# A rotary embedding on one core: three loads on SyncE's queue, and the software ring behind the sine table

## The chip, the cores and the metric

The kernel runs on 1 core of a Trainium2 chip. The metric is the device time of one execution in microseconds (us), as the median of several runs; a profile of one execution shows what each engine and each DMA queue did. The engines named here are VectorE (DVE), ScalarE (ACT), GpSimd (POOL) and SyncE (SP); TensorE has no work.

## The reference

The inputs are x of 8 x 2048 x 16 x 64 (batch, position, head, channel) and two tables of 2048 x 32, all float32. Each head's 64 channels are two halves that are rotated by the angle of the position:

```python
x1 = x[..., :head_dim // 2]
x2 = x[..., head_dim // 2:]
cos = cos[None, :, None, :]
sin = sin[None, :, None, :]
out1 = x1 * cos - x2 * sin
out2 = x1 * sin + x2 * cos
return np.concatenate([out1, out2], axis=-1)
```

So 67.1 MB are read and as many are written, for three elementwise operations on each element.

## The kernel before

One batch is one tile `xt` of 128 partitions. A partition holds J = 16 consecutive positions ("rows" here) of 16 heads and 64 channels, 16384 elements of float16. Five such buffers go round (`NBUF = 5`). GpSimd loads a batch with a DMA that turns float32 into float16 on its way (`load`, L54), VectorE rotates it in place with three operations of the whole tile (`rotate`: the product with sine at L75 into a scratch tile `v`, the product with cosine at L81, the sum at L83), and GpSimd stores it with a DMA that turns it back into float32 (`store`, L62; `store_rows`, L108). All of GpSimd's DMAs go through one software queue, q0 in the profile, which works them off in the order of issue. The kernel calls this order the ring, and writes it out by hand with order-only dependencies: load 0, the store of one row of batch 0, loads 1 to 4, and then stores and later loads in turn. A later load waits until the store of its buffer's last contents has landed.

The start is arranged by itself. The first two rows of batch 0 (`JA = 2`, the tile `head`, 1 MB in all) do not come with load 0 but as float32 by ScalarE's hardware queue (L44), behind the cosine table (L43); the sine table comes by SyncE's (L42). Load 0 brings the other 14 rows and waits for nothing. ScalarE narrows the tables to float16: sine into the upper half of `sin_h` (L94), its negative into the lower half (L95), cosine into `cos_h` (L96); then the head's first row and its second (`narrow_head`, L89, two calls). VectorE rotates the first row alone (`JF = 1`), GpSimd stores it (L108), and only behind that store come loads 1 to 4, of which the last takes the buffer that `head` had. The other 15 rows of batch 0 are rotated once load 0 has landed.

At the end, batch 7 goes out in three pieces: nine rows and five rows by GpSimd (L136, L138), and two rows that ScalarE widens (L147) and SyncE sends (L148) once the nine rows have landed.

Of the kernel before, what the change touches and what calls it, by code (L numbers as in the profile page):

```python
# [1 line left out]

# [4 lines left out]


@with_exitstack  # L10
def kernel(
    ctx: ExitStack,
    tc: tile.TileContext,
    x: bass.AP,
    cos: bass.AP,
    sin: bass.AP,
    out: bass.AP,
):
    nc = tc.nc
    f16 = mybir.dt.float16  # L20
    f32 = mybir.dt.float32

    B, S, H, D = x.shape
    Dh = D // 2
    P = nc.NUM_PARTITIONS
    J = S // P
    NBUF = 5

    const_pool = ctx.enter_context(tc.tile_pool(name="rope_const", bufs=1))
    io_pool = ctx.enter_context(tc.tile_pool(name="rope_io", bufs=NBUF))  # L30
    tmp_pool = ctx.enter_context(tc.tile_pool(name="rope_tmp", bufs=1))

    JA = 2
    JE = 2
    JF = 1
    head = io_pool.tile([P, JA, H, D], f32, tag="xt")
    x0 = x[0].rearrange("(p j) h d -> p j (h d)", j=J)
    sin_f = const_pool.tile([P, J, Dh], f32)
    cos_f = const_pool.tile([P, J, Dh], f32)
    cos_h = const_pool.tile([P, J, Dh], f16)  # L40
    sin_h = const_pool.tile([P, J, D], f16)
    nc.sync.dma_start(out=sin_f, in_=sin.rearrange("(p j) d -> p j d", j=J))  # L42
    nc.scalar.dma_start(out=cos_f, in_=cos.rearrange("(p j) d -> p j d", j=J))  # L43
    nc.scalar.dma_start(  # L44
        out=head.rearrange("p j h d -> p (j h d)"),
        in_=x0[:, 0:JA, :].rearrange("p j f -> p (j f)"),
    )

    loads = []

    def load(b):
        xt = io_pool.tile([P, J, H, D], f16, tag="xt")
        j0 = JA if b == 0 else 0
        dma = nc.gpsimd.dma_start(  # L54
            out=xt[:, j0:J, :, :].rearrange("p j h d -> p (j h d)"),
            in_=x[b].rearrange("(p j) h d -> p j (h d)", j=J)[:, j0:J, :].rearrange("p j f -> p (j f)"),
        )
        loads.append(dma)
        return xt

    def store(b, xt, j0=0):
        return nc.gpsimd.dma_start(  # L62
            out=out[b].rearrange("(p j) h d -> p j (h d)", j=J)[:, j0:J, :].rearrange("p j f -> p (j f)"),
            in_=xt[:, j0:J, :, :].rearrange("p j h d -> p (j h d)"),
        )

    def rotate(xt, j0, j1):
        v = tmp_pool.tile([P, J, H, D], f16)
        n = j1 - j0
        js = slice(j0, j1)  # L70
        shape = [P, n, H, 2, Dh]
        sin_b = sin_h[:, js, :].rearrange("p j (e d) -> p j e d", e=2).unsqueeze(2).to_broadcast(shape)
        cos_b = cos_h[:, js, :].unsqueeze(2).to_broadcast([P, n, 2 * H, Dh])
        xe = xt[:, js, :, :].rearrange("p j h (e d) -> p j h e d", e=2)
        nc.vector.tensor_mul(  # L75
            out=v[:, js, :, :].rearrange("p j h (e d) -> p j h e d", e=2),
            in0=xe[:, :, :, ::-1, :],
            in1=sin_b,
        )
        xw = xt[:, js, :, :].rearrange("p j h (e d) -> p j (h e) d", d=Dh)  # L80
        nc.vector.tensor_mul(out=xw, in0=xw, in1=cos_b)  # L81
        xa = xt[:, js, :, :].rearrange("p j h d -> p (j h d)")
        nc.vector.tensor_add(out=xa, in0=xa, in1=v[:, js, :, :].rearrange("p j h d -> p (j h d)"))  # L83


    tiles = [load(0)]

    def narrow_head(j0, j1):
        nc.scalar.copy(  # L89
            out=tiles[0][:, j0:j1, :, :].rearrange("p j h d -> p (j h d)"),  # L90
            in_=head[:, j0:j1, :, :].rearrange("p j h d -> p (j h d)"),
        )

    nc.scalar.copy(out=sin_h[:, :, Dh:D], in_=sin_f)  # L94
    nc.scalar.mul(out=sin_h[:, :, 0:Dh], in_=sin_f, mul=-1.0)  # L95
    nc.scalar.copy(out=cos_h, in_=cos_f)  # L96
    narrow_head(0, JF)
    narrow_head(JF, JA)
    rotate(tiles[0], 0, JF)
    def part(b, j0, j1):  # L100
        return (
            out[b].rearrange("(p j) h d -> p j (h d)", j=J)[:, j0:j1, :].rearrange("p j f -> p (j f)"),
            tiles[b][:, j0:j1, :, :].rearrange("p j h d -> p (j h d)"),
        )

    def store_rows(b, j0, j1):
        dst, src = part(b, j0, j1)
        return nc.gpsimd.dma_start(out=dst, in_=src)  # L108

    first = store_rows(0, 0, JF)  # L110
    ring = [loads[0], first]
    for b in range(1, NBUF):
        tiles.append(load(b))
        ring.append(loads[b])
    for a, b in zip(ring[1:], ring[:-1]):
        tc.add_manual_dep(
            a.ins,
            b.ins.name,
            mybir.DependencyInfo(mybir.DependencyClass.NoSync, mybir.DependencyReason.DATA),
            reason="order of the ring",  # L120
        )
    for b in range(B):
        rotate(tiles[b], JF if b == 0 else 0, J)
        if b < B - 1:
            st = store(b, tiles[b], JF if b == 0 else 0)
            if b == 0:
                tc.add_manual_dep(
                    st.ins,
                    first.ins.name,
                    mybir.DependencyInfo(mybir.DependencyClass.NoSync, mybir.DependencyReason.DATA),  # L130
                    reason="order of the ring",
                )
        if b + NBUF < B:
            tiles.append(load(b + NBUF))
    dst, src = part(B - 1, 0, 9)
    gate = nc.gpsimd.dma_start(out=dst, in_=src)  # L136
    dst, src = part(B - 1, 9, J - JE)
    rest = nc.gpsimd.dma_start(out=dst, in_=src)  # L138
    tc.add_manual_dep(
        rest.ins,  # L140
        gate.ins.name,
        mybir.DependencyInfo(mybir.DependencyClass.NoSync, mybir.DependencyReason.DATA),
        reason="order of the ring",
    )
    dst, src = part(B - 1, J - JE, J)
    tail = io_pool.tile([P, JE, H, D], f32, tag="xt")
    nc.scalar.copy(out=tail.rearrange("p j h d -> p (j h d)"), in_=src)  # L147
    end = nc.sync.dma_start(out=dst, in_=tail.rearrange("p j h d -> p (j h d)"))  # L148
    tc.add_manual_dep(
        end.ins,  # L150
        gate.ins.name,
        mybir.DependencyInfo(mybir.DependencyClass.Sync, mybir.DependencyReason.DATA),
        reason="the last rows go out behind this part",
    )


# [1 line left out]
_INS = ['x', 'cos', 'sin']  # L158
_OUTS = [((8, 2048, 16, 64), 'float32')]


# [23 lines left out]
```

## Time and profile before

| | us |
|---|---|
| median of 3 runs | 316.52 (316.48 to 316.58) |
| the profiled execution | 316.52 |
| its span | 314.7 |
| VectorE busy | 209.1 |
| ScalarE busy | 6.8 |
| load 0 (L54, 3584 KB), issue to landing | 22.7 |
| head (L44, 1024 KB), issue to landing | 12.0 |
| cosine (L43, 256 KB), issue to landing | 3.7 |
| sine (L42, 256 KB), issue to landing | 3.5 |

The span runs from the first to the last event that the profile shows; the execution's time is 1.8 us longer. In the rows of a timeline, ACTq, SPq and POOL with the operation DMA_DIRECT2D are issues of DMAs: their duration is that of issuing, not of moving the data. In the slices each digit is the busy share of one fortieth of the span, 7.9 us, in tenths. A row of the windows gives the stretch, its length, the busy time of VectorE, ScalarE and GpSimd with the number of their instructions, TensorE's granted clock, the busy share of the 16 DMA engines, and GB/s.

### The profile page before, as it was taken

The page shows a single profiled execution, that of the slowest core. Times are in us where ns is not written, and L with a number is a line of the kernel's source. Part 1 is how long each engine was busy: PE and PEld are TensorE (multiplying, and loading weights), DVE is VectorE, ACT ScalarE, POOL GpSimd, SP SyncE. Part 2 cuts the span into 40 slices and gives each one's busy share as a digit, 9 for nine tenths or more (in the row PEclk, how much of TensorE's full clock was granted, in tenths as well). Part 3 has the DMA queues.
Part 4 walks back from the last instruction along what each step waited for, and adds up shares of the span by engine and source line. Part 5 has one row for each costly group of instructions (what it writes and reads, how often), then busy time and mean ns, then how long its engine had stood idle before and what let it go on. Part 6 is the DMA issues. An engine that isn't in the chain of part 4 may idle for free.

```text
span 314.7 us, 125 instructions
## 1 busy us (share of the span) xinstructions
DVE 209.1 (66%) x27; ACT 6.8 (2%) x7; POOL 9.9 (3%) x22
## 2 busy tenths in 40 slices
DVE  0109999999999999999479999980009993000000
ACT  3200000000000000000000000000000002000000
POOL 1030000000000000010000000200000001000000
DMA  7989999999999899999999999999999999999998
GB/s 237 254 189 252 262 204 200 200 267 200 200 200 325 375 500 400 400 333 267 200 200 217 383 400 400 491 441 267 200 300 433 400 400 516 416 400 400 433 425 342
DMA packets 3168, 101.71 MB, mean 323 GB/s; under 512 B 352, under 2 KB 352, under 8 KB 736
## 3 DMA queue, kind: packets, MB, share of 16 engines
q0 software_dynamic: 2592, 99.09, 98.1%
q1 hardware_dynamic: 288, 1.31, 1.2%
q10 hardware_dynamic: 288, 1.31, 1.0%
HBM read 67.63 MB, written 67.11 MB: 428 GB/s over the span
## 4 chain that ended last, share of the span: by engine, by line
DVE 24%; issue 24%; DMA 19%; another core or an unknown queue 14%; POOL 1%; ACT 1%; DVEq 0%; POOLq 0%; PEldq 0%
DMA xt<-in_x_dram 19%; DVE v L75 8%; DVE xt L83 8%; DVE xt L81 8%; ACT tail L147 1%; POOL out_dram L62 1%; POOL xt L54 0%; DVEq L75 0%; POOLq L62 0%; PEldq L180 0%; POOLq L54 0%
## 5 line engine op out<-in xcount | busy, mean ns | idle before, releaser
L75 DVE TENSOR_TENSOR v<-xt,sin_h 128x16384 f16<-128x16384 f16 (+2 forms) x9 | 69.7, 7744 | 53.0 <-DMA xt<-in_x_dram 38.6
L83 DVE TENSOR_TENSOR xt<-xt,v 128x16384 f16<-128x16384 f16 (+2 forms) x9 | 69.7, 7744 | 0.3
L81 DVE TENSOR_TENSOR xt<-xt,cos_h 128x16384 f16<-128x16384 f16 (+2 forms) x9 | 69.7, 7744 | 0.3
L54 POOL DMA_DIRECT2D xt<-in_x_dram x8 | 4.4, 560 | 121.3 <-DMA out_dram<-xt 120.5
L147 ACT CAST tail<-xt 128x2048 f32<-128x2048 f16 x1 | 1.9, 1897 | 247.5 <-DVE xt L83 247.5
L62 POOL DMA_DIRECT2D out_dram<-xt x7 | 3.7, 535 | 67.2 <-DVE xt L83 67.2
L89 ACT CAST xt<-head 128x1024 f16<-128x1024 f32 x2 | 2.0, 1042 | 7.3 <-DMA head<-in_x_dram 7.3
L136 POOL DMA_DIRECT2D out_dram<-xt x1 | 0.5, 531 | 50.6 <-DVE xt L83 50.6
L94 ACT ACT_TABLE_LOAD x1 | 1.3, 1283 | 1.7 <-PEq L169 1.7
L108 POOL DMA_DIRECT2D out_dram<-xt x1 | 0.5, 531 | 14.8 <-DVE xt L83 14.8
L94 ACT CAST sin_h<-sin_f 128x512 f16<-128x512 f32 x1 | 0.6, 617 | 1.3 <-DMA sin_f<-in_sin_dram 1.3
L95 ACT ACTIVATE sin_h<-sin_f 128x512 f16<-128x512 f32 x1 | 0.6, 624 | 0.0
L96 ACT CAST cos_h<-cos_f 128x512 f16<-128x512 f32 x1 | 0.6, 601 | 0.0
L138 POOL DMA_DIRECT2D out_dram<-xt x1 | 0.5, 531 | 0.0
L169 POOL MEMSET const-float32-0.0<- 128x1 f32 x1 | 0.1, 98 | 0.2 <-issue 0.2
L169 POOL MEMSET const-bfloat16-1.0<- 128x1 bf16 x1 | 0.1, 101 | 0.0
L169 POOL MEMSET const-float32-1.0<- 128x1 f32 x1 | 0.1, 98 | 0.0
L169 POOL MEMSET const-uint8-127<- 128x1 uint8 x1 | 0.1, 98 | 0.0
## 6 DMA issues: line engine op xcount, KB each, us to landing
xt<-in_x_dram POOLq DMA_DIRECT2D x7, 4096.0 KB, 38.4
out_dram<-xt POOLq DMA_DIRECT2D x1, 7680.0 KB, 71.8
out_dram<-xt POOLq DMA_DIRECT2D x1, 4608.0 KB, 42.4
xt<-in_x_dram POOLq DMA_DIRECT2D x1, 3584.0 KB, 22.7
out_dram<-xt POOLq DMA_DIRECT2D x1, 2560.0 KB, 47.9
head<-in_x_dram ACTq DMA_DIRECT2D x1, 1024.0 KB, 12.0
out_dram<-tail SPq DMA_DIRECT2D x1, 1024.0 KB, 8.4
out_dram<-xt POOLq DMA_DIRECT2D x1, 512.0 KB, 8.5
```

What stands on the lines that cost most here:

```text
L54: dma = nc.gpsimd.dma_start(out=xt[:, j0:J, :, :].rearrange("p j h d -> p (j h d)"), in_=x[b].rearrange("(p j) h d -> p j (h d)", j=J)[:, ...
L62: return nc.gpsimd.dma_start(out=out[b].rearrange("(p j) h d -> p j (h d)", j=J)[:, j0:J, :].rearrange("p j f -> p (j f)"), in_=xt[:, j0:J ...
L75: nc.vector.tensor_mul(out=v[:, js, :, :].rearrange("p j h (e d) -> p j h e d", e=2), in0=xe[:, :, :, ::-1, :], in1=sin_b,)
L81: nc.vector.tensor_mul(out=xw, in0=xw, in1=cos_b)
L83: nc.vector.tensor_add(out=xa, in0=xa, in1=v[:, js, :, :].rearrange("p j h d -> p (j h d)"))
L89: nc.scalar.copy(out=tiles[0][:, j0:j1, :, :].rearrange("p j h d -> p (j h d)"), in_=head[:, j0:j1, :, :].rearrange("p j h d -> p (j h d)"),)
L94: nc.scalar.copy(out=sin_h[:, :, Dh:D], in_=sin_f)
L95: nc.scalar.mul(out=sin_h[:, :, 0:Dh], in_=sin_f, mul=-1.0)
L96: nc.scalar.copy(out=cos_h, in_=cos_f)
L108: return nc.gpsimd.dma_start(out=dst, in_=src)
L136: gate = nc.gpsimd.dma_start(out=dst, in_=src)
L147: nc.scalar.copy(out=tail.rearrange("p j h d -> p (j h d)"), in_=src)
```

## The change

SyncE's queue now carries all three hardware loads of the start, in the order sine, head, cosine; ScalarE issues none. ScalarE narrows the head's first row ahead of cosine. And load 0, the first transfer of the software ring, gets a dependency on ScalarE's first narrowing of sine (L94), with a semaphore, so that GpSimd issues it only after that instruction. The order of instructions on VectorE and on GpSimd stays as it was; VectorE's first product with cosine waits for ScalarE in addition.

```diff
     nc.sync.dma_start(out=sin_f, in_=sin.rearrange("(p j) d -> p j d", j=J))
-    nc.scalar.dma_start(out=cos_f, in_=cos.rearrange("(p j) d -> p j d", j=J))
-    nc.scalar.dma_start(
+    nc.sync.dma_start(
         out=head.rearrange("p j h d -> p (j h d)"),
         in_=x0[:, 0:JA, :].rearrange("p j f -> p (j f)"),
     )
+    nc.sync.dma_start(out=cos_f, in_=cos.rearrange("(p j) d -> p j d", j=J))
...
-    nc.scalar.copy(out=sin_h[:, :, Dh:D], in_=sin_f)
+    sine = nc.scalar.copy(out=sin_h[:, :, Dh:D], in_=sin_f)
     nc.scalar.mul(out=sin_h[:, :, 0:Dh], in_=sin_f, mul=-1.0)
+    narrow_head(0, JF)
     nc.scalar.copy(out=cos_h, in_=cos_f)
-    narrow_head(0, JF)
     narrow_head(JF, JA)
...
     first = store_rows(0, 0, JF)
+    tc.add_manual_dep(
+        loads[0].ins,
+        sine.ins.name,
+        mybir.DependencyInfo(mybir.DependencyClass.Sync, mybir.DependencyReason.DATA),
+        reason="the rows of SyncE's queue go ahead of the ring",
+    )
     ring = [loads[0], first]
```

## The prediction

> **What bounds the kernel now.** I read the page's slices first, then the queue table, the DMA issues, the timeline of the first 30 us, the waits, and last the packet records of the trace (start, duration, queue and size of each DMA packet), because the slices say that the DMA engines are the limit and only the packets show where they stand idle.
>
> The page, busy tenths and queues:
>
> ```profile
> DVE  0109999999999999999479999980009993000000
> DMA  7989999999999899999999999999999999999998
> q0 software_dynamic: 2592, 99.09, 98.1%
> q1 hardware_dynamic: 288, 1.31, 1.2%
> q10 hardware_dynamic: 288, 1.31, 1.0%
> ```
>
> The DMA row is full from the second slice to the last, while VectorE has long empty stretches. The three shares sum to 100.3% because packets overlap by some 20 ns; laid end to end on 16 engines, the packets leave no hole over 0.15 us after 4.3 us, and the last ones end at 313.2 to 313.5 us. So from 4.3 us on the time is a sum of DMA packets, nearly all on the software queue (q0), which runs in the order of GpSimd's issues. A hole made in it is never refilled.
>
> The timeline of the start (start, duration, in brackets idle before and releaser):
>
> ```profile
> 0.73 0.40 ACTq L43 DMA_DIRECT2D cos_f<-in_cos_dram  x1
> 0.73 0.37 SPq L42 DMA_DIRECT2D sin_f<-in_sin_dram  x1
> 1.17 0.46 ACTq L44 DMA_DIRECT2D head<-in_x_dram  x1
> 1.25 0.67 POOL L54 DMA_DIRECT2D xt<-in_x_dram  x1 [0.81 <-PEq L180]
> 1.65 1.28 ACT L94 ACT_TABLE_LOAD   x1 [1.65 <-PEq L169]
> 4.23 0.62 ACT L94 CAST sin_h<-sin_f 128x512 f16<-128x512 f32 x1 [1.29 <-DMA sin_f<-in_sin_dram]
> 13.22 1.99 ACT L89 CAST xt<-head 128x1024 f16<-128x1024 f32 x2 [7.33 <-DMA head<-in_x_dram]
> 16.75 0.53 POOL L108 DMA_DIRECT2D out_dram<-xt  x1 [14.83 <-DVE xt L83]
> 24.04 8.16 DVE L75 TENSOR_TENSOR v<-xt,sin_h 128x15360 f16<-128x15360 f16 x1 [7.60 <-DMA xt<-in_x_dram]
> ```
>
> GpSimd issues load 0 at 1.25 us and waits for nothing. The change makes it wait for the cast at 4.23. One-microsecond windows (DMA share counts a packet where it starts, so values over 1 are long packets starting):
>
> ```profile
> 1.50:2.50 1.00, 0.00 (x0) 0.85 (x1) 0.41 (x1) 1.00 0.71 66
> 2.50:3.50 1.00, 0.00 (x0) 0.43 (x1) 0.00 (x0) 1.00 0.84 328
> 3.50:4.50 1.00, 0.00 (x0) 0.27 (x1) 0.00 (x0) 1.00 1.14 467
> 4.50:5.50 1.00, 0.00 (x0) 1.00 (x3) 0.00 (x0) 1.00 1.00 426
> 5.50:6.50 1.00, 0.00 (x0) 0.39 (x1) 0.00 (x0) 1.00 2.19 483
> ```
>
> In the packet records, sine's packets begin at 1.75 us, cosine's at 2.75, the head's (8 per engine, 8 KB, 309 ns each) at 3.72. Load 0's first packets (8 per engine, 28 KB, 2129 ns each) begin on all engines at 5.55 to 5.93. That is 4.31 us after GpSimd's issue began, although the engines had been serving the hardware queues one by one until then; from 5.55 on software and head packets alternate. So load 0 had nothing ready before 5.55, and the hardware packets have until now filled exactly the time that its start takes.
>
> **The change, part by part.** Only the start of load 0 can move the end; I follow it.
>
> 1. Sine. SyncE's issue stays first, at 0.73, and landed at 4.21. Cosine now comes last instead of in parallel. From 2.75 on cosine's packets (8 per engine, about 80 ns apart) held about half of the engines; sine's packets still needed some 0.49 us of engine time at 2.75 and took until about 3.75. Alone they are done by 3.25, so sine lands at about 3.7, 0.5 earlier. Bounds: 3.55 (all 0.64 us of cosine saved) to 4.21 (nothing). I take 3.7, since the overlap is seen in the records.
>
> 2. ScalarE loses its two issues (0.40 + 0.46 us); its table load (1.28) moves forward to about 0.7 and ends near 2.0, before sine is there. Nothing gained on the path; if it slipped back to its old end at 2.94 it would still be covered by sine's landing. The cast runs 3.72 to 4.34.
>
> 3. The added wait. GpSimd started 0.28 to 0.30 us after VectorE's end where it waited for it (74.77 to 75.06, 16.44 to 16.75); I take 0.28 after ScalarE: load 0 is issued at 4.62, not 1.25. Behind the wait on GpSimd stand the first store (L108) and loads 1 to 4. They have to be issued only before load 0's packets run out, at about 26 us, and the store comes at about 9.6 (step 5): covered by 16 us.
>
> 4. From issue to first packet. No other software transfer of this trace starts on an empty queue, so there is a single row, 4.31 us, and it is that of this very instruction. Below, the nearest row is SyncE's sine, 1.02 us from issue to first packet. Above, 4.31 us plus a wait-related extra that I can't see. I take 4.31, because it is the same instruction, the first on its queue in both kernels. First packets then at 8.93.
>
> The hardware packets: at 5.55 each engine still had two head packets (2 x 0.32 us) to serve. With load 0 away they follow at once, so sine, head and cosine are all done at about 5.55 + 0.64 = 6.19; the order of cosine and head changes nothing in that sum. From 6.19 to 8.93 the engines have nothing: 2.74 us lost.
>
> In words of the Trainium skill (DMA: Bandwidth & Descriptors, Latency and other measured facts) a GpSimd-issued DMA brings its first byte after about 1 us, the hardware path after 0.6; the rows here, 4.31 and 1.02, are both longer. By the page's figure load 0 would start at 5.6, before the head is done, and the sum would be zero.
>
> 5. What comes earlier and brings nothing. The head lands near 6.1 instead of 13.1 (landing follows the last packet by about 0.37), narrowing (1.04) ends at 7.1, and the narrowing of cosine (0.60, now behind the first half of the head) near 7.7. VectorE's three small products (3 x 0.69, the second waiting for cosine) end near 9.3, the first store is issued at 9.6 rather than 16.75. But its packets follow load 0 in q0 and began at 23.5 right behind it before; they do so again, 2.7 us later. SyncE has nothing behind its two added issues until the tail at 305.
>
> 6. What comes later and costs nothing more. VectorE's large products start when load 0 lands (24.04, then 26.8). The covers are these: the store issued at 48.88 is reached by q0 only when load 4 has landed (102.5), 53 us; the last tile is done at 262.7 while the stores ahead of it land at 294.5, 32 us. Each load that waits for a buffer (121.2, 140.2, 198.2) has a whole 19.3 us transfer in the queue ahead of it. All of these shift together.
>
> Sum: +2.74 us on the profiled execution's 316.52 us (span 314.7 and 1.8 around it), which equals the median of the runs: 319.3. Bounds with 4.31 kept: sine at 3.55 gives +2.6, at 4.21 gives +3.25.
>
> **The rivals.** A measurement of this kernel can tell about 0.2%, 0.63 us, from no change.
>
> (a) *The latency shrinks.* Part of 4.31 us may be paid by the clock or by company: the three hardware requests show their first packets at 1.75, 2.75 and 3.72, one microsecond apart, as if served in turn, and load 0 is the fourth; and its issue took 667 ns against 531 to 567 later. After 4.6 us it would be alone. Against it: GpSimd shows nothing at work on this transfer before 1.25, and descriptors that are ready earlier would have had their turn earlier. Every microsecond saved is one off the loss. With 2.2 to 3.8 us the result is +0.65 to +2.2 (about 317.9 in the middle).
>
> (b) *No hole at all.* If the start takes under 1.6 us (6.19 - 4.62), as sine's 1.02 does, load 0 reaches the engines before the head is through; the sum of packets is then unchanged: 316.5. Up to 2.2 us of latency it stays within 0.63 us. Against it stands the one row of this instruction, 4.31 us. The 1 us that the Trainium skill (DMA: Bandwidth & Descriptors, Latency and other measured facts) gives for this path would bring this case about; no run so far shows it.
>
> (c) *Faster.* The first 32 sine packets, two per engine, took up to 855 ns where the others take 84: the window 1.75 to 2.57 carries work for 0.17 us and so loses 0.65. If that came from two queues being set up at once, it could vanish when SyncE asks alone, and everything moves forward by up to 0.65: 315.9. It decides only if (b) holds too; else the 2.74 swallows it. Against it: cosine's packets had not begun then, so more likely it is the first touch of the memory, which stays.
>
> (d) *The change does nothing*, if the wait were over before GpSimd gets there. It can't be: the issue now stands at 1.25 and the cast cannot end before 4.1.
>
> **How the numbers follow.** Forecast (+2.4 to +3.5): 0.62. (a): 0.20. (b) with the part of (a) that stays inside 0.63 us: 0.14. (c): 0.03, and 0.01 for (d) or an unseen mishap that leaves it the same. Faster 0.03, same 0.14 and slower 0.83, rounding the last hundredth to slower. The range leaves out (b), (c) and the lowest end of (a), under 2 in 10: from 317.2 to 320.0, the top being the forecast's +3.25 and 0.2 for a later wake of GpSimd.
>
> **What would show it.** Step 1: the first narrowing of sine starts near 3.7. Step 3: load 0's issue at 4.6. Step 4: a window of about 6.3 to 8.8 us with a DMA share near 0, and load 0's landing near 26.6 instead of 23.9, so about 22.0 us after its issue. Step 5: the head's narrowing near 6.1 and the first store's issue near 9.6. Step 6: every later row moved by the same 2.7, busy sums of VectorE and of q0 unchanged. I am wrong if load 0's first packets come under 4 us after its issue, if a hole shows up later in the DMA row or one of before disappears, or if the end moves by another amount than load 0's landing.

## The result, and the profile after

The changed kernel takes 318.88 us (median of 6 runs, 318.67 to 319.73) against 316.50 (6 runs, 316.47 to 316.58): a ratio of 1.0079, 95% interval 1.0069 to 1.0090, or 2.4 us more. The profiled execution took 318.89 us, its span is 317.1.

The slices and queues of the changed kernel's page:

```profile
DVE  0106999999999999999669999990008994000000
DMA  9999999999999999999999999999999999999896
q0 software_dynamic: 2592, 99.09, 97.7%
q1 hardware_dynamic: 576, 2.62, 2.2%
```

The software queue carries the same 2592 packets and 99.09 MB. The DMA row stays full, and the end is still a sum of packets; one hardware queue now has what two had. The start in its timeline:

```profile
0.74 0.37 SPq L42 DMA_DIRECT2D sin_f<-in_sin_dram  x1
1.16 0.42 SPq L43 DMA_DIRECT2D head<-in_x_dram  x1
1.64 0.42 SPq L47 DMA_DIRECT2D cos_f<-in_cos_dram  x1
3.67 0.62 ACT L94 CAST sin_h<-sin_f 128x512 f16<-128x512 f32 x1 [1.65 <-DMA sin_f<-in_sin_dram]
4.60 0.67 POOL L54 DMA_DIRECT2D xt<-in_x_dram  x1 [4.15 <-ACT sin_h L94]
6.00 1.04 ACT L89 CAST xt<-head 128x1024 f16<-128x1024 f32 x1 [1.17 <-DMA head<-in_x_dram]
9.61 0.53 POOL L108 DMA_DIRECT2D out_dram<-xt  x1 [4.34 <-DVE xt L83]
26.41 8.16 DVE L75 TENSOR_TENSOR v<-xt,sin_h 128x15360 f16<-128x15360 f16 x1 [17.11 <-DMA xt<-in_x_dram]
```

Load 0 is issued at 4.60, 3.35 us later than before. VectorE gets its rows at 26.41, 2.37 us later than before (24.04), and the execution is 2.37 us longer: 318.89 - 26.41 = 316.52 - 24.04 = 292.48. All that the change does is done by the time load 0 has landed. Windows of the start, with columns as before:

```profile
4.50:5.50 1.00, 0.00 (x0) 0.32 (x1) 0.67 (x1) 1.00 0.92 383
5.50:6.50 1.00, 0.00 (x0) 0.51 (x1) 0.00 (x0) 1.00 1.73 412
6.50:7.50 1.00, 0.43 (x1) 1.00 (x3) 0.00 (x0) 1.00 1.61 258
7.50:8.50 1.00, 0.89 (x2) 1.00 (x2) 0.00 (x0) 1.00 0.13 29
```

No window is empty: long packets start in the one from 5.5 to 6.5 and in the next (the 0.13 from 7.5 to 8.5 is the engines at work on them). By the packet records, the hardware packets end at 6.0 to 6.3, and the 16 engines take their first packet of load 0 one after the other from 6.31 to 7.77, 1.71 to 3.17 us after the issue. Between its last hardware packet and its first of load 0 an engine stood empty for 0.56 us on average. There was no hole of 2.7 us, yet 2.4 us were lost.

### The profile page after: what moved, and what is told of

Its sections match the earlier page's. It is cut to its first block, busy times and chain, and to the rows that moved or that the text cites. A ratio compares the mean times of both kernels' runs of the same rounds, so it can differ in the third digit from the quotient of the medians.

```text
span 317.1 us, 126 instructions
## 1 busy us (share of the span) xinstructions
DVE 209.1 (66%) x27; ACT 6.8 (2%) x7; POOL 9.9 (3%) x22
## 3 DMA queue, kind: packets, MB, share of 16 engines
q0 software_dynamic: 2592, 99.09, 97.7%
q1 hardware_dynamic: 576, 2.62, 2.2%
## 4 chain that ended last, share of the span: by engine, by line
DVE 24%; issue 24%; DMA 20%; another core or an unknown queue 14%; POOL 1%; ACT 1%; DVEq 0%; POOLq 0%
DMA xt<-in_x_dram 19%; DVE xt L81 8%; DVE v L75 8%; DVE xt L83 8%; DMA sin_f<-in_sin_dram 1%; ACT tail L153 1%; POOL out_dram L62 0%; POOL xt L54 0%; ACT sin_h L94 0%; DVEq L75 0%; POOLq L62 0%; POOLq L54 0%
## 5 line engine op out<-in xcount | busy, mean ns | idle before, releaser
L75 DVE TENSOR_TENSOR v<-xt,sin_h 128x16384 f16<-128x16384 f16 (+2 forms) x9 | 69.7, 7744 | 55.3 <-DMA xt<-in_x_dram 48.1
L94 ACT CAST sin_h<-sin_f 128x512 f16<-128x512 f32 x1 | 0.6, 617 | 1.6 <-DMA sin_f<-in_sin_dram 1.6
```

Source lines behind the costliest of these rows:

```text
L75: nc.vector.tensor_mul(out=v[:, js, :, :].rearrange("p j h (e d) -> p j h e d", e=2), in0=xe[:, :, :, ::-1, :], in1=sin_b,)
L94: sine = nc.scalar.copy(out=sin_h[:, :, Dh:D], in_=sin_f)
```

## The experiments

Theory A: the wait costs, because load 0 must now start on engines that run empty. Theory C: asking by one queue costs. B and D are two accounts of the 4.31 us from issue to first packet in the kernel before: a latency that holds for any start, or a fixed time. All ratios are against runs of the kernel before on the same chip (medians 316.48 to 316.58).

### The parts one by one

The wait alone, on the kernel before:

```diff
-    nc.scalar.copy(out=sin_h[:, :, Dh:D], in_=sin_f)
+    sine = nc.scalar.copy(out=sin_h[:, :, Dh:D], in_=sin_f)
...
+    tc.add_manual_dep(loads[0].ins, sine.ins.name, ...)
```

> The kernel before with the wait alone: queues as before (cosine and head on ScalarE's queue), load 0 waits for the first narrowing of sine. Theory A (the wait costs: a software transfer that starts on idle DMA engines needs 1.7 us from its issue to its first packet on the first engine and about 3.2 on the last, its first packets are longer, and the engine that loses most sets the end): the cast ends at 4.85, load 0 is issued at 5.1, half a microsecond later than in the changed kernel, first packets from 6.8 on, time 319.4 (318.7 to 320.0). Theory C (asking by one queue costs, not the wait): 316.5.

Measured: 317.99, ratio 1.0044 (1.0029 to 1.0059). Load 0 was issued at 5.38, first packets at 6.76 to 7.78. The wait costs 1.4 us by itself, so A holds in direction; but it costs less than the whole change, although load 0 is issued 0.8 us later. That is below A's range (318.7 to 320.0) and not what any theory said; C, which had 316.5, is out as the whole account.

The queues alone, the changed kernel without the dependency:

```diff
-    tc.add_manual_dep(loads[0].ins, sine.ins.name, ...)
```

> The changed kernel without the wait: SyncE asks for sine, head and cosine, the order of narrowing as in the change, load 0 issued at once. Theory A: the DMA engines are never empty after the start, 316.5 (316.2 to 316.9), with head and cosine late because they alternate with load 0. Theory C: about 318.9, as the changed kernel.

Measured: 322.12, ratio 1.0175 (1.0160 to 1.0190), 5.5 us slower than before and slower than the whole change. Both theories missed. Its timeline shows why:

```profile
8.26 1.04 ACT L89 CAST xt<-head 128x1024 f16<-128x1024 f32 x1 [3.65 <-DMA head<-in_x_dram]
23.88 0.62 ACT L97 CAST cos_h<-cos_f 128x512 f16<-128x512 f32 x1 [14.58 <-DMA cos_f<-in_cos_dram]
26.26 0.53 POOL L108 DMA_DIRECT2D out_dram<-xt  x1 [24.35 <-DVE xt L83]
26.79 2.14 POOL L54 DMA_DIRECT2D xt<-in_x_dram  x4
```

and its windows:

```profile
23.00:24.00 1.00, 0.00 (x0) 0.12 (x1) 0.00 (x0) 1.00 0.10 33
24.00:25.00 1.00, 0.47 (x1) 1.00 (x2) 0.00 (x0) 1.00 0.00 0
25.00:26.00 1.00, 0.92 (x2) 0.45 (x1) 0.00 (x0) 1.00 0.00 0
26.00:27.00 1.00, 0.96 (x1) 0.00 (x0) 0.74 (x2) 1.00 0.00 0
27.00:28.00 1.00, 1.00 (x1) 0.00 (x0) 1.00 (x3) 1.00 0.83 291
```

Cosine, asked for last, takes turns with load 0: each of its 8 small packets per engine lets a 2.13 us packet of load 0 pass, and it lands only with load 0, at 23.8. VectorE's second product waits for it, the first store for VectorE, and loads 1 to 4 stand behind that store on GpSimd. Load 0 has run out by then, and the DMA engines stand still from about 23.4 to 27.4. So the two halves of the change don't add up: the order of asking is affordable only with the wait, which lets the three hardware loads through first.

To see whether cosine's place or the single queue does it, cosine was asked for second and the head last, without a wait:

```diff
     nc.sync.dma_start(out=sin_f, ...)
+    nc.sync.dma_start(out=cos_f, ...)
     nc.sync.dma_start(out=head..., ...)
-    nc.sync.dma_start(out=cos_f, ...)
...
-    tc.add_manual_dep(loads[0].ins, sine.ins.name, ...)
```

> SyncE asks for sine, cosine and head, and load 0 waits for nothing. If the queues without the wait were slow (322.1) because cosine, asked for last, alternated with load 0's 28 KB packets and held up the first store and loads 1 to 4: cosine lands by 5, the head by 13 to 18, the first store is issued before load 0 lands, 316.5 (316.2 to 317.0). If one queue instead of two is what costs: 318 or more.

Measured: 323.54, ratio 1.0222 (1.0205 to 1.0240). The expectation failed: cosine came early, but now the head is last, and load 0's first packets came from 3.37 us on, ahead of all of the head's. Its timeline (of an execution of 325.24 us):

```profile
4.54 0.62 ACT L97 CAST cos_h<-cos_f 128x512 f16<-128x512 f32 x1
25.77 1.99 ACT L89 CAST xt<-head 128x1024 f16<-128x1024 f32 x2 [20.61 <-DMA head<-in_x_dram]
29.30 0.53 POOL L108 DMA_DIRECT2D out_dram<-xt  x1 [27.38 <-DVE xt L83]
```

Whatever SyncE asks for third, at 1.63 or 1.64, meets load 0 and is held until 24 to 26 us. In the kernel before, with two queues, the last request (the head) was issued at 1.17, and six of its eight packets per engine passed before load 0's first.

### Load 0 by itself

The kernel before, with sine, cosine and head asked for only after load 0 has landed:

```diff
+    tiles = [load(0)]
+    for ask in asks:          # the three hardware loads, issued behind it
+        tc.add_manual_dep(ask.ins, loads[0].ins.name, ...)
```

> The kernel before, but sine, cosine and head are asked for only once load 0 has landed, so that load 0 starts at 1.25 us with nothing else on the DMA engines. Its total is longer by the late start of VectorE's first row and is not what is compared. Theory A (in the kernel before load 0 was ready from about 3 us on and stood behind packets of the head that the engines had already taken in): first packets at 2.9 to 4.5 us. Theory B or D (load 0 is ready only at 5.5, 4.31 us after its issue or at a fixed time): first packets at 5.5.

Measured: one run, 326.85. Its windows:

```profile
0.50:1.50 1.00, 0.00 (x0) 0.00 (x0) 0.25 (x1) 1.00 0.00 0
1.50:2.50 1.00, 0.00 (x0) 0.00 (x0) 0.41 (x1) 1.00 0.00 0
2.50:3.50 1.00, 0.00 (x0) 0.00 (x0) 0.00 (x0) 1.00 2.85 459
```

Issued at 1.25 like in the kernel before, load 0 had its first packets on all engines at 2.61 to 3.41, 1.37 to 2.16 us after the issue. So the 4.31 us were no latency of the software queue: B and D are out. In the kernel before, load 0's first packets came only behind hardware packets. Whether it was ready by then and had to wait its turn, or whether its start itself takes longer beside them, no run separates. Its first packet on an engine is longer here: 2.85 us on average instead of 2.13.

In words of the Trainium skill (DMA: Bandwidth & Descriptors, Latency and other measured facts) this path has its first byte after about 1 us; the 1.37 us measured here decide, and are nearer to it than the 4.31 of the kernel before. The same page of the Trainium skill (Queues, rings and completion order) says that a DMA engine goes round its queues packet by packet; the trace of before agrees from 5.55 us on, and shows no turn for load 0 ahead of that, though here it had its packets by 3.4.

### Later and earlier waits

Load 0 waiting for the narrowing of the head's first row:

```diff
-        sine.ins.name,
+        head_row.ins.name,      # narrow_head(0, JF)
```

> The changed kernel with load 0 waiting for the narrowing of the head's first row instead of that of sine, which ends 2.7 us later (7.04 instead of 4.29). Theory A: load 0 issued at 7.3, first packets at 9.0 to 10.5, every microsecond of the wait is now lost in full, so 318.9 + 2.7 = 321.6 (321.0 to 322.3). Theory B (the prediction's 4.31 us from issue to first packet holds for a transfer that starts alone): first packets at 11.6. Theory D (the start of the software queue is tied to the clock, not to the issue): first packets stay near 6.3 to 7.8 or follow the issue by well under 1.7 us, time under 320.

Measured: 320.05, ratio 1.0107 (1.0091 to 1.0124). Issue at 7.47, first packets at 8.85 to 9.47: 1.37 to 2.00 after it, as when load 0 is alone, and neither B's 11.6 nor D. But the time is 1.5 us under A's: the wait grew by 2.9 us and the time by 1.2. So something in the change itself costs more than its late issue.

A second profile of the changed kernel, to look at the engines one by one:

> The changed kernel once more, for a second profile. Theory S (the slowest of the 16 DMA engines sets the end, and in the changed kernel one or two engines start load 0 about a microsecond behind the rest): load 0's completions again spread over 1 us or more (24.7 to 26.3 in the first profile), and the time of the profiled execution follows the last completion, not the mean: time minus last completion 292.6 as in the first profile. If the spread was an accident: under 0.5 us, and a time near 318.0.

Measured: 319.01 (318.63 to 319.31), ratio 1.0076 (1.0061 to 1.0091). The 16 completions of load 0, read here as one per DMA engine, came from 24.50 to 26.71, a spread of 2.2 us; before they lay within 0.28 (23.63 to 23.91). VectorE's row and the execution followed the last of them:

```profile
26.83 8.16 DVE L75 TENSOR_TENSOR v<-xt,sin_h 128x15360 f16<-128x15360 f16 x1 [17.48 <-DMA xt<-in_x_dram]
```

319.31 - 26.83 = 292.48 again. And an engine that is late stays late: load 4 lands over a spread of 2.2 us as well (103.06 to 105.30), and so does the very last transfer (314.44 to 316.68). The records do not name the engine, but this is what is seen if each engine has its own share of every transfer, and the slowest of the 16 carries its delay to the end. Theory S holds. What makes engines late? Cosine ahead of the head, with the wait:

> The changed kernel, but SyncE asks for cosine ahead of the head (and cosine is narrowed ahead of it), wait on sine as in the change. Load 0 is still issued at about 4.6, and the same bytes go ahead of it; only the last hardware packets beside its start are the head's 8 KB ones instead of cosine's 2 KB ones. Theory S with cosine's packets as the cause of the late engines: spread under 0.5 us, first packets done by 9.2, time 317.5 (317.2 to 318.0). Theory S with any hardware packets as the cause: 318.9 as the changed kernel. Theory H (the time follows the issue of load 0 alone): 318.9.

(The order of asking as in the run with cosine second, the dependency kept.) Measured: 319.45, ratio 1.0089 (1.0072 to 1.0106). Spread 1.96 us, first packets from 6.03 to 9.08. So the spread does not need cosine's small packets, which had landed by 4.1; here the head's last packets, held back until 9.1, met load 0's first. The comparison is not clean, since the head itself was slow.

Load 0 waiting for the second narrowing of sine:

```diff
-    sine = nc.scalar.copy(out=sin_h[:, :, Dh:D], in_=sin_f)
-    nc.scalar.mul(out=sin_h[:, :, 0:Dh], in_=sin_f, mul=-1.0)
+    nc.scalar.copy(out=sin_h[:, :, Dh:D], in_=sin_f)
+    sine = nc.scalar.mul(out=sin_h[:, :, 0:Dh], in_=sin_f, mul=-1.0)
```

> The changed kernel with load 0 waiting for the second narrowing of sine (the negative one), 0.53 us later: issue at 5.1, first packets from 6.5 on, when cosine's packets are over. Theory H: 0.5 us more, 319.4. Theory S with cosine's packets as the cause: the engines start together, no slower than the changed kernel in spite of the later issue, 318.0 (317.6 to 318.6).

Measured: 318.38 (317.70 to 318.82), ratio 1.0054 (1.0038 to 1.0071). Not slower for the later issue, against H, and inside the range of S, but not for S's reason: the engines did not start together. In the profiled execution (issue 4.87, first packets from 6.27, hardware packets until 6.42) the two still met, and the spread was still 1.5. Further delays, by ScalarE instructions with a scratch result:

```diff
+    for _ in range(1):        # 2 in the other kernel
+        sine = nc.scalar.mul(out=scratch, in_=sin_f, mul=-1.0)
```

> The changed kernel with one more ScalarE instruction on sine (its result goes to a scratch tile that nobody reads), on which load 0 waits: issue at 5.4, 0.8 to 1.0 later than in the change. The hardware packets end at 6.2 as before, load 0's first come from 6.7 on, so the two no longer meet. Theory S2 (engines start unevenly where the first software packets meet the last hardware packets, and evenly where these are over): spread of load 0's completions under 0.7 us, time 318.0 (317.6 to 318.4), faster than the changed kernel by 0.9 in spite of the later issue. Theory H (the time follows the issue): 319.7.

> The same with two such instructions: issue at 5.9. Theory S2: spread under 0.7 us as well, and the half microsecond is now lost in full: 318.5 (318.1 to 318.9), on the line through 5.38 us, 318.0 (wait alone) and 7.47 us, 320.05 (wait on the head's row). If the unevenness has another cause: spread over 1 us, 319.5 or more.

Measured: 318.20, ratio 1.0053 (1.0038 to 1.0068), and 318.93, ratio 1.0077 (1.0062 to 1.0092). The first is faster than the changed kernel by 0.7 us, with the issue 0.8 later; the second loses those 0.7 us again, with an issue at 6.14, and ends just above S2's 318.9. The first one's issue and VectorE's start:

```profile
5.44 0.67 POOL L55 DMA_DIRECT2D xt<-in_x_dram  x1 [5.00 <-ACT scratch L98]
25.79 8.16 DVE L76 TENSOR_TENSOR v<-xt,sin_h 128x15360 f16<-128x15360 f16 x1 [16.25 <-DMA xt<-in_x_dram]
```

The profiled executions of the kernel before and of every kernel in which all of load 0 waits, in us (the spread is that of the 16 completions):

| load 0 waits for | issue | last hardware packet ends | first packets | completions | spread | VectorE's L75 starts | time |
|---|---|---|---|---|---|---|---|
| nothing (before) | 1.25 | engines never empty | 5.55-5.93 | 23.63-23.91 | 0.3 | 24.04 | 316.52 |
| sine (changed, again) | 4.36 | 6.29 | 6.14-7.81 | 24.50-26.71 | 2.2 | 26.83 | 319.31 |
| sine, cosine ahead of the head | 4.53 | 9.08 | 6.03-9.08 | 25.00-26.96 | 2.0 | 27.09 | 319.52 |
| sine (changed) | 4.60 | 6.32 | 6.31-7.77 | 24.67-26.28 | 1.6 | 26.41 | 318.89 |
| second narrowing | 4.87 | 6.42 | 6.27-7.31 | 24.62-26.08 | 1.5 | 26.20 | 318.63 |
| sine, queues of before | 5.38 | 6.64 | 6.76-7.78 | 25.00-25.40 | 0.4 | 25.53 | 318.00 |
| one scratch more | 5.44 | 6.55 | 6.81-7.56 | 25.14-25.67 | 0.5 | 25.79 | 318.27 |
| two scratch more | 6.14 | 6.37 | 7.51-8.44 | 25.80-26.32 | 0.5 | 26.44 | 318.91 |
| head's first row | 7.47 | 6.39 | 8.85-9.47 | 27.06-27.68 | 0.6 | 27.80 | 320.28 |

Time minus VectorE's start is 292.4 to 292.5 in every row. In the rows with a wait, the spread is 1.5 us or more where load 0's first packet comes no later than the last hardware packet ends, and at most 0.6 where it comes later. An early issue as such does not do it: load 0 alone, issued at 1.25, lands with a spread of 0.6 (20.48 to 21.07). Nor does company as such: in the kernel before, load 0 runs beside head packets until 12.9, and its spread is 0.3. In the uneven rows load 0 begins while the hardware queues run out. Not all of the spread comes from the start: in the changed kernel the engines are 1.2 us apart at the end of the seventh packet of load 0 and 1.7 at the end of the eighth, with the wait on the second narrowing 1.0 and 1.4. Why the engines fall apart when the two meet is not shown; S2 names the condition, not the mechanism.

From 5.4 us on, each microsecond of the issue costs about one of time: (320.28 - 318.27) / (7.47 - 5.44) = 0.99.

### Filling the hole

The changed kernel, with two of load 0's 14 rows as a transfer of their own that waits for nothing:

```diff
+        if b == 0:
+            j0 = JA + 2
+            early.append(nc.gpsimd.dma_start(out=xt[:, JA:j0, ...], in_=x0[:, JA:j0, :]...))
...
-    ring = [loads[0], first]
+    ring = [early[0], loads[0], first]
```

> The changed kernel with two rows of load 0 as a software transfer of their own that waits for nothing (issued at 1.25), the other 12 rows waiting for sine as load 0 does in the change. The first piece gives each DMA engine 8 packets of about 0.3 us, 2.4 us of work, more than the hole. Theory A (the change costs the time in which the engines are empty or start anew before load 0): the engines never run dry, 316.6 (316.2 to 317.1), with cosine landing by about 9. If it is the wait on GpSimd or the later issue itself that costs: 318 or more.

Measured: 316.59 (10 runs), ratio 1.0000 (0.9990 to 1.0009). In its timeline the rest of load 0 still waits for sine, and VectorE still starts on time:

```profile
4.40 0.54 POOL L61 DMA_DIRECT2D xt<-in_x_dram  x1 [2.49 <-ACT sin_h L101]
11.05 0.62 ACT L104 CAST cos_h<-cos_f 128x512 f16<-128x512 f32 x1 [3.65 <-DMA cos_f<-in_cos_dram]
24.08 8.16 DVE L82 TENSOR_TENSOR v<-xt,sin_h 128x15360 f16<-128x15360 f16 x1 [10.96 <-DMA xt<-in_x_dram]
```

The two rows fill the time in which the rest starts, the loss is gone, and the wait on GpSimd as such costs nothing. Cosine came later than expected, its narrowing at 11.05 against a landing by about 9, and that cost nothing either. This is no faster than the kernel before, and no version here is: from 2.9 to 30 us the kernel before always has 16 or more packets at work, as many as there are DMA engines, so there is no idle time there to give back.

## Why the prediction was right or wrong

The direction, the place and the size came out: 319.3 forecast, 318.88 measured, inside the range. The frame holds: the time after load 0's landing is the same to 0.1 us in every kernel in which the first store is early enough, and a delay of load 0 is never made good. One of the terms that made up the 2.74 us was wrong, though, and another that I left out took its place.

Steps 1 to 3 held. Sine was narrowed at 3.67 (3.72 said) and load 0 issued at 4.60 (4.62). The table load moved to 0.74 and cost nothing. (What sine still needed at 2.75 comes to 0.42 us by the packet records, not 0.49; that shifts step 1 by less than 0.1.)

Step 4 failed. I took 4.31 us for the time from an issue on GpSimd to its first packet, because it was the only row. The run with load 0 alone shows 1.37 to 2.16, and the first engine's 1.37 us came again in all four waiting kernels whose hardware packets were over by then. In the kernel before the rest was time behind head packets. My argument that load 0 "had nothing ready before 5.55", since an earlier descriptor would have had its turn, does not hold: software packets came from 3.37 us on where the head was asked for later. So the latency did as rival (a) has it, and it came nearly to (b): the 1.71 us of the first engine are 0.1 over the 1.6 that (b) has free; only the last engine's 3.17 are 1.6 over it. But neither rival has the time: the 16 engines' mean of 2.12 us from issue to first packet would have lost about 0.55 by the prediction's sum, not 2.37.

What the 2.37 us consist of, from the packet records of the two profiles. The 16 first packets start on average at 6.72 instead of 5.72, and 0.64 of that 1.00 is the two head packets that now go ahead: 0.36 are left. Load 0's eight packets take 18.18 us per engine instead of 17.19: 0.99, of which 0.71 is the first packet (2.84 on average instead of 2.13). That is 1.35 for the average engine. The remaining 1.02 us is what the slowest engine fell further behind the average (1.22 us instead of 0.19 at the landing), which the prediction did not have: it treated the 16 engines as one. The sum was near the forecast by the accident that these two terms came to about what the false latency gave.

The hole that step 4 foresaw, a DMA share near 0 from 6.3 to 8.8, is not there; the sign of being wrong that the prediction named ("load 0's first packets come under 4 us after its issue") told it. Load 0's landing (26.6 said, 26.3 measured) could not, and alone would have confirmed a wrong step.

Step 5 held (head narrowed at 6.00, first store at 9.61), and it is more than "brings nothing": without the wait the cover of 16 us that I gave the first store would have been gone. I had not costed the two parts apart; alone they cost 1.4 and 5.5 us, together 2.4. Step 6 held: VectorE's busy time is 209.1 in both, q0 has the same packets.

Rival (c), faster, had little in it: with SyncE asking alone, the first 32 packets of sine still took up to 616 ns (855 before), together 0.59 us per engine instead of 0.71. That is 0.12 us of the 0.65 that (c) hoped for. Whether the rest is the first touch of the memory, as the prediction guessed, no run shows.

## What to carry to other kernels

Where a profile's DMA row is full, as here, follow the slowest DMA engine's last completion, not the mean: an engine that starts a transfer late carries its delay to the end. A time from issue to first packet that was measured while other queues were busy is not a latency; measure it on empty engines before you build a sum on it. Where a small transfer is to overtake a large one, look at which of them the engines have in line first: here the third request on one queue was overtaken by 28 KB packets, and a wait that cost 1.4 us alone saved 3.2 us when it was added to that order.

## What the runs showed of the hardware

Three things were not expected. The first packet of a software transfer on empty engines took 2.62 to 2.88 us on average (2.85 with load 0 alone), where the second to the seventh took 2.13 to 2.18; in the kernel before, where it follows head packets without a gap, it took 2.13. The 16 engines began load 0 within 0.6 to 1.0 us of each other where nothing was left of the hardware queues, but 1.0 to 1.7 apart where the last hardware packets were just ending, and 3.0 where the head's were still going; in the kernel before, whose engines were never empty, 0.4. And an earlier issue made the kernel slower between 4.4 and 5.4 us: 318.88 at 4.60, 318.20 at 5.44 (the runs of the two do not overlap: 318.67 to 319.73 and 318.02 to 318.27). The cause of the unevenness behind it stays open; the packet records do not name the engine.
